# Four part reads of the scores' blocks, and one block transposition in place of two, in an RWKV-7 trunk layer

## The chip, the cores and the metric

The kernel runs on one core of one Trainium2 chip. The metric is device time in microseconds (us) of one execution, as the median of several. The engines are named as in the profile: PE (TensorE, matmuls), PEld (its weight loads), DVE (VectorE), ACT (ScalarE), POOL (GpSimd) and SP (SyncE, which issues most of the DMAs). An engine works through its own queue in order; a row of a profile is one instruction or a run of like ones.

## The reference, cut to what matters

One layer of a residual trunk over 512 tokens and 2048 features, all in float32. Half of the features go through 16 RWKV-7 heads of 64, the other half through a pooling branch; both are gated, projected, added to the residual, gated again by a per-layer embedding and normalised.

```python
h = rms_norm(x, norm_g[i]);  z = h @ w_in[i]              # 512 x 2048 by 2048 x 6272
zs = zs + (token_shift(zs) - zs) * mu[i]                   # r, k, v, two lora inputs
decay = exp(-exp(-softplus(-(w0 + tanh(wd) @ w_up)) - 0.5));  a = sigmoid(a0 + ad @ a_up)
kk = k * k_k;  kk = kk / max(norm(kk per head), KK_EPS);  k = k * (1 + (a - 1) * k_a)
# per head, per token t:
sa  = S @ -kk_t
S   = S * w_t + sa kk_t a_t + v_t k_t;   y_t = S @ r_t
y = head_group_norm(y) + bonus;  y_rwkv = y * silu(g_rwkv)
d = causal_multiscale_pool(u);   y_pool = (d @ w_pool) * pool_scale * silu(g_pool)
x = x + concat(y_rwkv, y_pool) @ w_out
x = x + sigmoid(x @ w_pg + b_pg) * (p @ w_ple);   return rms_norm(x, final_g)
```

## The kernel before, in words

Every large product is done as three products of float32r halves (`whi`, `wlo` of a weight; `hhi`, `hlo` of the activations), so each weight tile that SP loads (`raw`, 256 KB, four buffers) is split by ACT (`whi`, line 132) and then by DVE (`wlo`, line 133) before PE can use it. The buffers of `raw` come free when `wlo` is made, those of `whi` when PE has used them: the split of one chunk therefore waits on ACT until PE is through with the chunk four before it.

The 16 heads are worked as eight pairs, j = 0 to 7, of 128 partitions. The sequence is cut into eight chunks of 64 tokens, and the token recurrence is turned into a chunk recurrence. For a pair there are these stages, and they overlap across pairs:

- `prepare_key(j)` and `norm_key(j)`: the squared key `kk` is split into `kqh` (ACT, line 140) and `kql` (DVE, line 141), and two matmuls `pss` with the block matrix `blk` sum it per head: the first reads `kqh`, the second `kql`. For j of 2 and more this is done inside `recur(j - 2)`, `pss` at its chunk 5, and ACT copies the sum out (line 576).
- `scores(j)`: 32 matmuls `pm` and four masked copies `mt`; then the 32x32 diagonal blocks of the strictly triangular matrices are written to DRAM (`nd`, four DMAs, line 677) and read back as `n32`, two tiles of 16 rows each (`n` in the rows), in which each of four groups of 32 partitions holds the same 32 blocks (line 682). After them SP has `load_ab` (`ur`, `ar`), `bg` and `vg` for later stages.
- `invert(j)`: DVE inverts the 32 blocks by 31 steps of a multiply `tm` (line 709) and an add `xw` (line 713). The first tile of `n32` is needed by the first step, the second by step 16. For j of 1 and more the steps are handed out a few at a time within `recur(j - 1)`, and DVE's queue has other work behind each. The result goes to DRAM (`xd`) and back into `x1` (four DMAs, line 724).
- `gather(j)`: the corner blocks of `x1` are transposed on DVE (`y1`, line 777) and PE forms the off-diagonal blocks of the inverse: 32 small matmuls `pq`, one reading each block and head, then `pmv` and `px`.
- `recur(j)`: for each of eight chunks a chain PE `py`, DVE `zs` (line 844), PE `pu`, ACT `uv` (line 858), PE `ps`, DVE `sbd` (lines 872 and 874), and again. Between the links PE gets `pump(n)` matmuls of the input projections `zk`, `zr`, `zv`, `zg`, `zb` as filling.

After the last pair come the output projection (`acc_o`), the gate projection (`acc_g`) and the closing norm, where PE alone sets the pace.

Who sets the order: PE's instructions are pinned to the order of the code until the last pair is done. Those of DVE, ACT and SP are put into their queues by the framework's planner when the program is built, by its own estimate of when each can begin; `issue_after` holds one instruction behind another, `high_priority` lifts the links of the chain. So an edit of a DMA or of one instruction can move others of the same queue. SP uses its DMA semaphores in turn, and its rows show waits for an earlier DMA's landing before a later issue.

Of the kernel before, what the change touches and what calls it, by code (L numbers as in the profile page):

```python
# [34 lines left out]
def trunk_kernel(ctx: ExitStack, tc: tile.TileContext, x, p, norm_g, w_in, mu, w0, w_up, a0, a_up,  # L35
                 k_k, k_a, r_k, ln_w, ln_b, w_pool, pool_scale, w_out, w_ple, w_pg, b_pg, final_g, out):
    nc = tc.nc
    PSUM = bass.MemoryType.PSUM
    x, p, w_in, w_out, w_ple, w_pg = x[0], p[0, 0], w_in[0], w_out[0], w_ple[0], w_pg[0]
    out = out[0]  # L40
# [118 lines left out]
    def mm(*a, **k):  # L159
        i = nc.tensor.matmul(*a, **k)  # L160
        return tc.keep_in_program_order(i) if pin[0] else i

    def tr(*a):
        i = nc.tensor.transpose(*a)
        return tc.keep_in_program_order(i) if pin[0] else i
# [30 lines left out]
    n_ = 0  # L196
# [13 lines left out]
    for kind, nm, j in jobs:  # L210
# [7 lines left out]
        else:  # L218
            g, i = j // 4, j % 2
# [79 lines left out]
    for d in range(KT):  # L299
        xt_half(0, d)  # L300
        if d in WPOS:
            c = len(wl_)
# [18 lines left out]
    for g, win in enumerate(WINDOWS):  # L321
        t_ = cst.tile([P, win], F32, name=f"rc{g}")
# [61 lines left out]
    for nm, rows in (("u", slice(0, 64)), ("a", slice(64, 128))):  # L384
# [3 lines left out]
        t_ = rw.tile([P, T], F32R, name=f"{nm}hh")  # L388
# [257 lines left out]
    def scores(j):  # L646
        ar, bk, v_ = (st_[j][n_] for n_ in ("ar", "bk", "v_"))
        kph, kpl = st_[j].pop("kp")

        mt = rw.tile([P, 2, 8, 2, C], F32, name=f"mt{j}", tag="mt", bufs=2)  # L650
        pm = [[psM.tile([P, T], F32, name=f"pm{j}_{par}0", tag="m"),
               psY.tile([P, T], F32, name=f"pm{j}_{par}1", tag="y")] for par in range(2)]
        for par in range(2):
            for q in range(4):
                for h in range(2):
                    rows = slice(64 * h, 64 * h + 64)
                    mm(pm[par][h][:, q * P:(q + 1) * P], bk[rows, q, 2 * par:2 * par + 2, :],
                       ar[rows, q, 2 * par:2 * par + 2, :], start=True, stop=True)
        for par in range(2):
            for h in range(2):  # L660
                nc.vector.tensor_tensor(mt[:, par, h::2, :, :],
                                        pm[par][h].rearrange("p (u a t) -> p u a t", u=4, a=2),
                                        msk[:, par:par + 2, :].unsqueeze(1).to_broadcast([P, 4, 2, C]), ALU.mult)


        ps = psM.tile([P, T], F32, name=f"pbo{j}", tag="m")
        mm(ps, blk, kph, start=True, stop=False)
        mm(ps, blk, kpl, start=False, stop=True)
        bv = rw.tile([P, T], F32, name=f"bv{j}", tag="bv", bufs=2)
        nc.vector.tensor_tensor(bv, ps, v_, ALU.mult)  # L670

        nd = dram.tile([2, 2, 8, 32, 32], F32, name=f"nd{j}", tag="nd")
        for par in range(2):
            pb = 64 * (1 - par)
            for b in range(2):
                rows = slice(pb + 32 * b, pb + 32 * b + 32)
                nc.sync.dma_start(out=nd[par, b].rearrange("u r c -> r u c"),
                                  in_=mt[rows, par, :, 1 - par, 32 * b:32 * b + 32])
        nb = []
        for i in range(2):  # L680
            t_ = rw.tile([P, 16, 32], F32, name=f"n32{j}_{i}", tag=("kk", "kp")[i])
            n_ = nc.sync.dma_start(out=t_, in_=nd[:, :, :, 16 * i:16 * i + 16, :].rearrange(
                "a b u r c -> (a b u) r c").unsqueeze(0).to_broadcast([4, 32, 16, 32]))
            nb.append(t_)
        if j + 1 < NJ:
            with tc.issue_after(n_.ins):
                load_ab(j + 1)
        bg = rw.tile([P, NCH, 4, 32], F32, name=f"bg{j}", tag="bk")
        with tc.issue_after(n_.ins):
            for q in range(4):  # L690
                nc.sync.dma_start(out=bg[32 * q:32 * q + 32],
                                  in_=st_[j]["bkd"].rearrange("(b k) (c q i) -> q k c b i", b=4, q=4, i=32)[q])
        if j:
            vg, vd = vgs[j]
            with tc.issue_after(n_.ins):
                for q in range(4):
                    nc.sync.dma_start(out=vg[32 * q:32 * q + 32],
                                      in_=vd.rearrange("(b k) (c q i) -> q k c b i", b=4, q=4, i=32)[q])
        st_[j].update(mt=mt, nb=nb, bv=bv, bg=bg)
# [30 lines left out]
    def gather(j):  # L730
        d = st_[j]
        v_, mt = d.pop("v_"), d["mt"]
        if j + 1 < NJ:
            if j == 0:
                prepare_key(1)
            decay_and_rate(j + 1)

        uv = rw.tile([P, NCH, P], F32, name=f"uv{j}", tag="uv")
        if j:
            vg, _ = vgs.pop(j)  # L740
            for h in range(2):
                hr = slice(64 * h, 64 * h + 64)
                nc.vector.transpose(uv[hr, h::2, :].rearrange("p c (b k) -> p c b k", k=32), vg[hr])
        else:
            ps = psY.tile([P, T], F32, name=f"pv{j}", tag="y")
            for tt in range(NT):
                tr(ps[:, tt * P:(tt + 1) * P], v_[:, tt * P:(tt + 1) * P], ident)
            pv = ps.rearrange("p (t c) -> p t c", c=P)
            nc.scalar.copy(uv[0:64, 0::2, :], pv[0:64])
            nc.scalar.copy(uv[64:128, 1::2, :], pv[64:128])  # L750


        if j == 0:
            turn_key(0, 0)
            turn_key(0, 1)
        pump(H4)

        d.update(uv=uv)
        if j == 0:
            norm_key(1)  # L760
        if 0 < j < NJ - 1:
            with tc.issue_after(read[-1].ins):
                spread_norm(j + 1)
        pump(H5)
        pump(HX)

        x1 = d["x1"]

        def units(fn):
            for u in range(8):  # L770
                for par in range(2):
                    fn(u, par, 64 * (1 - par))

        y1 = rw.tile([P, 8, 32], F32, name=f"y1{j}", tag="tm")

        with tc.issue_after(late[0].ins):
            yt = [nc.vector.transpose(y1[pb:pb + 32], x1[pb:pb + 32, :, 0:32]) for pb in (0, 64)]
        with tc.issue_after(yt[0].ins), tc.issue_after(yt[1].ins):
            if normed:
                normed.pop()()  # L780
            if j + 1 < NJ:
                scale_key(j + 1)
        ps3 = psM.tile([P, 8, 32], F32, name=f"pq2{j}", tag="m")
        units(lambda u, par, pb: mm(ps3[pb + 32:pb + 64, u, :],
                                                  mt[pb:pb + 32, par, u, 1 - par, 32:64],
                                                  y1[pb:pb + 32, u, :], start=True, stop=True,
                                                  tile_position=(pb, pb + 32)))
        q2t = rw.tile([P, 8, 32], F32, name=f"q2{j}", tag="xw")
        with tc.high_priority(offset=HP):
            for pb in (0, 64):  # L790
                nc.scalar.copy(q2t[pb + 32:pb + 64], ps3[pb + 32:pb + 64])
        psv = psM.tile([P, 8, C], F32, name=f"pmv{j}", tag="m")
        units(lambda u, par, pb: mm(psv[pb:pb + 64, u, :], mt[64 - pb:128 - pb, par, u, 1 - par, :],
                                    uv[64 - pb:128 - pb, 2 * (u // 2) + par, 64 * (u % 2):64 * (u % 2) + 64],
                                    start=True, stop=True))
        ps4 = psM.tile([P, 8, 32], F32, name=f"px2{j}", tag="m")
        units(lambda u, par, pb: mm(ps4[pb:pb + 32, u, :], q2t[pb + 32:pb + 64, u, :],
                                                  x1[pb + 32:pb + 64, u, 32:64], start=True, stop=True,
                                                  tile_position=(pb + 32, pb)))
        for pb in (0, 64):  # L800
            nc.scalar.copy(x1[pb:pb + 32, :, 32:64], ps4[pb:pb + 32])
        mv = rw.tile([P, 4, P], F32, name=f"mv{j}", tag="mv")
        nc.scalar.copy(zsp[0][64:128, :].rearrange("p (h t) -> p h t", h=2), psv[64:128, 0:2, :])
        nc.scalar.copy(mv.rearrange("p q (h t) -> p (q h) t", h=2), psv)
        d["mv"] = mv
        pump(H1)
        if pending:
            gates.append(pending.pop()())
        pump(H1)
# [150 lines left out]
    prepare(0)  # L960
    pump(H3)
    scores(0)
    pump(H2)
    for _ in invert(0):
# [3 lines left out]
    for j in range(NJ):  # L968
# [6 lines left out]
        if j + 1 == NJ:  # L975
            pn.append(rw.tile([P, 2, T // 32, 32], F32, name="pn", tag="ar", bufs=2))
            for q in range(4):
                for c in range(2):
                    nc.sync.dma_start(out=pn[0][32 * q:32 * q + 32, c],
                                      in_=p[:, c * P + 32 * q:c * P + 32 * q + 32].rearrange("(b k) i -> k b i", k=32))  # L980
# [93 lines left out]
    for ec in range(D // EC):  # L1074
# [3 lines left out]
        for tt in range(NT):  # L1078
            rows = slice(tt * P, (tt + 1) * P)
            t_ = pp.tile([P, EC], F32, name=f"x2_{ec}_{tt}", tag=("u", "sw")[tt // 2])  # L1080
# [3 lines left out]
                                in_=t_.rearrange("p (c e) -> p c e", e=P))  # L1084
# [204 lines left out]
```

## Time and profile before

| what | before |
|---|---|
| median of 3 runs | 1072.54 us (1072.24 to 1074.22) |
| the profiled execution, its own time | 1077.76 us |
| its span, first to last instruction | 1076.0 us |
| mean granted TensorE clock | 0.997 |
| PE busy | 1047.7 us, 97% |
| DVE busy | 711.7 us, 66% |
| ACT busy | 435.0 us, 40% |
| PE busy in 0 to 27 us | 15.09 us |
| PE busy in 702 to 1076 us | 365.26 of 374 us |

The profiled execution is 5.22 us over the median of the runs, and 1.76 us of its time lies outside the span. A timeline row gives the start, the length, the engine, the line, the operation, out<-in, the shapes and the count; the bracket at its end is the idle time of that engine just before and what ended it. A row of the table of waits gives the sum, the number of times and the longest wait.

### The profile page before, as it was taken

Reading aid. Unit: us, or ns where it says so; the run is one execution under the profiler, and the core shown is the slowest. Engines: PE = TensorE matmul, PEld = TensorE weight load, DVE = VectorE, ACT = ScalarE, POOL = GpSimd, SP = SyncE. Lnnn points to the kernel's source line nnn. Section 1 sums busy time; section 2 is a strip of 40 time slices with the busy share of each in tenths; the row PEclk is TensorE's granted clock in tenths of the full one; section 3 lists DMA queues with packets and bytes.
Section 4 is the critical chain, followed back from the end, with each engine's and each line's share of the span. In section 5 each row is a group of like instructions: output and inputs, shape, how many; then the busy total and the mean of one; then the engine's idle time right before and its main releaser. Section 6 shows DMA issues by size and latency. Waiting matters only on the chain.

```text
span 1076.0 us, 17131 instructions
## 1 busy us (share of the span) xinstructions
PE 1047.7 (97%) x5912; PEld 864.6 (80%) x5912; DVE 711.7 (66%) x1879; ACT 435.0 (40%) x893; POOL 72.6 (7%) x180
## 2 busy tenths in 40 slices
PE   5999999999999999999999999999999999999996
PEld 4888878888877887888888788888888888888885
DVE  6676968878688689687786977464353344435356
ACT  7633424434334345253443344544232232324337
POOL 2100011010110110101101201000000000000000
PEclk9999999999999999999999999999999999999998
DMA  7434453453443544534544453775747659454534
GB/s 237 110 115 101 135 132 95 130 139 99 143 116 100 160 105 128 128 95 133 132 118 133 112 130 108 225 259 163 183 152 190 163 145 272 129 177 159 173 98 157
DMA packets 272733, 155.41 MB, mean 144 GB/s; under 512 B 114449, under 2 KB 235386, under 8 KB 272646
## 3 DMA queue, kind: packets, MB, share of 16 engines
q1 hardware_dynamic: 244630, 125.74, 42.2%
q10 hardware_dynamic: 28016, 28.58, 8.8%
q8 instruction: 46, 0.75, 0.3%
q14 instruction: 41, 0.34, 0.1%
HBM read 128.79 MB, written 24.95 MB: 143 GB/s over the span
## 4 chain that ended last, share of the span: by engine, by line
PE 81%; DVE 9%; DMA 5%; ACT 2%; issue 2%; SPq 1%; ACTq 0%; DVEq 0%
PE acc_o L160 16%; PE acc_g L160 16%; PE zb L160 10%; PE zv L160 7%; PE zr L160 7%; PE zg L160 6%; PE zk L160 6%; PE py L160 2%; PE pple L160 2%; DMA n<-nd 1%; PE pu L160 1%; PE pm L160 1%; DMA x<-xd 1%; PE pp L160 1%; PE ps L160 1%
## 5 line engine op out<-in xcount | busy, mean ns | idle before, releaser
L133 DVE TENSOR_TENSOR wlo_g<-raw_g,whi_g 128x512 fp32r<-128x512 f32 x84 | 57.1, 687 | 76.0 <-ACT whi_g L132 73.8
L160 PE MATMUL zb<-hhi,whi_b 128*128 128x512 f32 x256 | 105.5, 412 | 0.0
L160 PE MATMUL zb<-hhi,wlo_b 128*128 128x512 f32 x256 | 100.4, 392 | 0.0
L160 PE MATMUL zb<-hlo,whi_b 128*128 128x512 f32 x256 | 99.8, 390 | 0.0
L160 PE MATMUL acc_o<-wlo_o,yhi 128*128 128x512 f32 x256 | 99.6, 389 | 0.0
L160 PE MATMUL acc_o<-whi_o,ylo 128*128 128x512 f32 x256 | 99.6, 389 | 0.0
L133 DVE TENSOR_TENSOR wlo_o<-raw_o,whi_o 128x512 fp32r<-128x512 f32 x64 | 43.9, 690 | 81.0 <-ACT whi_o L132 72.8
L160 PE MATMUL acc_o<-whi_o,yhi 128*128 128x512 f32 x256 | 94.7, 389 | 0.0
L132 ACT CAST whi_g<-raw_g 128x512 fp32r<-128x512 f32 x84 | 51.9, 620 | 103.0 <-PE acc_g L160 57.4
L160 PE MATMUL acc_g<-whi_g,x2hi 128*128 128x512 f32 x208 | 81.1, 390 | 0.0
L160 PE MATMUL acc_g<-wlo_g,x2hi 128*128 128x512 f32 x208 | 81.0, 389 | 0.0
L160 PE MATMUL acc_g<-whi_g,x2lo 128*128 128x512 f32 x208 | 80.7, 390 | 0.0
L881 POOL TENSOR_SCALAR s0p<-sbd,pw 64x64 f32<-64x64 f32 x96 | 56.4, 587 | 336.6 <-DVE sbd L874 245.1
L132 ACT CAST whi_o<-raw_o 128x512 fp32r<-128x512 f32 x64 | 39.5, 621 | 96.1 <-PE acc_o L160 55.0
L132 ACT CAST whi_b<-raw_b 128x512 fp32r<-128x512 f32 x64 | 39.6, 620 | 75.9 <-PE zb L160 22.4
L713 DVE TENSOR_TENSOR xw<-xw,tm 128x60 f32<-128x60 f32 (+24 forms) x248 | 52.2, 210 | 7.1
L160 PEld LDWEIGHTS zb<-hhi,wlo_b 128*128 128x128 f32 x256 | 48.0, 188 | 10.8
L160 PEld LDWEIGHTS acc_o<-whi_o,ylo 128*128 128x128 f32 x256 | 48.1, 188 | 10.1
L160 PEld LDWEIGHTS acc_o<-whi_o,yhi 128*128 128x128 f32 x256 | 48.0, 188 | 10.0
L160 PEld LDWEIGHTS acc_o<-wlo_o,yhi 128*128 128x128 f32 x256 | 48.0, 188 | 9.9
L133 DVE TENSOR_TENSOR wlo_b<-raw_b,whi_b 128x512 fp32r<-128x512 f32 x64 | 43.7, 684 | 17.8 <-ACT whi_b L132 17.2
L160 PEld LDWEIGHTS zb<-hhi,whi_b 128*128 128x128 f32 x256 | 48.2, 188 | 8.6
(289 smaller groups left out, 2502.2 us busy)
## 6 DMA issues: line engine op xcount, KB each, us to landing
raw_b<-in_w_in_dram SPq DMA_DIRECT2D x64, 256.0 KB
raw_o<-in_w_out_dram SPq DMA_DIRECT2D x64, 256.0 KB
raw_g<-in_w_pg_dram SPq DMA_DIRECT2D x64, 256.0 KB
raw_k<-in_w_in_dram SPq DMA_DIRECT2D x32, 256.0 KB
raw_r<-in_w_in_dram SPq DMA_DIRECT2D x32, 256.0 KB
raw_v<-in_w_in_dram SPq DMA_DIRECT2D x32, 256.0 KB
raw_g<-in_w_in_dram SPq DMA_DIRECT2D x32, 256.0 KB
bkd<-bk SPq DMA_DIRECT2D x8, 512.0 KB
```

Of the source, the lines that this page charges most:

```text
L132: made.append(nc.scalar.copy(hi, raw))
L133: made.append(nc.vector.tensor_tensor(lo, raw, hi.bitcast(F32), ALU.subtract))
L160: i = nc.tensor.matmul(*a, **k)
L713: nc.vector.tensor_tensor(xw[:, 0:n_, s + 1:32], xw[:, 0:n_, s + 1:32], tm[:, 0:n_, 0:w_], ALU.add)
L881: nc.gpsimd.tensor_scalar(s0p[hc, :], nxt[hc, hc], pcn[hc], None, ALU.mult)
```

## The change

Two edits. In `scores`, each of the two reads of `nd` that fill 128 partitions by a broadcast over four groups is replaced by four reads of 32 partitions each with the same source. In `gather`, the two transpositions of 32 partitions each (of partitions 0 to 31 and 64 to 95) are replaced by one over all 128; the half of its output that is new is read by nothing.

```diff
@@ scores
             t_ = rw.tile([P, 16, 32], F32, name=f"n32{j}_{i}", tag=("kk", "kp")[i])
-            n_ = nc.sync.dma_start(out=t_, in_=nd[:, :, :, 16 * i:16 * i + 16, :].rearrange(
-                "a b u r c -> (a b u) r c").unsqueeze(0).to_broadcast([4, 32, 16, 32]))
+            for q in range(4):
+                n_ = nc.sync.dma_start(out=t_[32 * q:32 * q + 32], in_=nd[:, :, :, 16 * i:16 * i + 16, :].rearrange(
+                    "a b u r c -> (a b u) r c"))
@@ gather
-            yt = [nc.vector.transpose(y1[pb:pb + 32], x1[pb:pb + 32, :, 0:32]) for pb in (0, 64)]
-        with tc.issue_after(yt[0].ins), tc.issue_after(yt[1].ins):
+            yt = nc.vector.transpose(y1, x1[:, :, 0:32])
+        with tc.issue_after(yt.ins):
```

The line numbers behind line 682 are one higher in the changed kernel. PE's and POOL's queues keep their order. In the other three the planner has moved instructions; three places follow.

SP's queue at `scores(3)`; `n` are the reads, `raw_r` and `raw_v` weight chunks, `ur` a lora weight. Before:

```order
L677 DMA nd_3715<-mt_3685 32x8x32 x4
L129 DMA raw_r_2_2113<-in_w_in_dram 128x4x128
L682 DMA n_0_3720<-nd_3715 128x1x512
L682 DMA n_1_3722<-nd_3715 128x1x512
L357 DMA ur_3724<-in_w_up_dram 64x128 x2
L129 DMA raw_r_3_2119<-in_w_in_dram 128x4x128
```

and now:

```order
L677 DMA nd_3730<-mt_3700 32x8x32 x4
L129 DMA raw_r_2_2124<-in_w_in_dram 128x4x128
L683 DMA n_0_3735<-nd_3730 32x512 x3
L129 DMA raw_r_3_2130<-in_w_in_dram 128x4x128
L683 DMA n_0_3735<-nd_3730 32x512
L683 DMA n_1_3740<-nd_3730 32x512 x2
L129 DMA raw_v_0_2156<-in_w_in_dram 128x4x128
```

The last quarter of the first tile now stands behind a weight chunk. So it does in every pair but one: in `scores(1)` all four stand ahead of the chunk.

ACT's queue in `recur(0)`, around `norm_key(2)`; `kqh` is the high half of the squared key, `kk<-pss` the copy of the sum. Before:

```order
L132 CAST whi_v_0_1316<-raw_v_0_1314 128x512
L140 CAST kqh_2094<-kk_2092 128x512
L858 COPY uv_1458<-pu_5_2131 64x64 x2
L132 CAST whi_v_1_1334<-raw_v_1_1332 128x512
L576 COPY kk_2092<-pss_2160 128x512
```

and now:

```order
L132 CAST whi_v_0_1322<-raw_v_0_1320 128x512
L859 COPY uv_1464<-pu_5_2142 64x64 x2
L132 CAST whi_v_1_1340<-raw_v_1_1338 128x512
L140 CAST kqh_2105<-kk_2103 128x512
L576 COPY kk_2103<-pss_2171 128x512
```

`kqh` has moved behind the `uv` copies and the next split of a weight, to just ahead of the copy that reads its matmuls' sum. The same has happened in `recur(1)` to `recur(5)`; in `recur(2)` and `recur(3)` it is also behind the ACT pass of the shifted `sr`. On DVE `kql` has moved along, from behind the split `wlo_v_0` to behind `wlo_v_1` (in `recur(2)` behind DVE's `sr` as well), just ahead of the `sbd` of that chunk.

DVE's queue at `gather(0)`. Before:

```order
L574 TENSOR_SCALAR kk_1429<-pss_1489 128x512
L777 STREAM_TRANSPOSE y_1548<-x_1150 32x256 x2
L595 RECIPROCAL kk_1429<-kk_1429 128x512
L133 TENSOR_TENSOR wlo_b_2_1065<-raw_b_2_1062,whi_b_2_1064 128x512
L133 TENSOR_TENSOR wlo_b_3_1159<-raw_b_3_1156,whi_b_3_1158 128x512
L373 SCALAR_TENSOR_TENSOR sv_1523<-zv_1383,prm,sv_1523 128x511
```

and now:

```order
L574 TENSOR_SCALAR kk_1435<-pss_1495 128x512
L614 TENSOR_SCALAR tha_1462<-tha_1462 128x512
L615 TENSOR_TENSOR ar_1641<-sr_1386,pw_1454 128x4x2x64
L617 TENSOR_TENSOR bk_1642<-kp_1643,ipw_1455 128x4x2x64
L133 TENSOR_TENSOR wlo_b_2_1071<-raw_b_2_1068,whi_b_2_1070 128x512
L618 SCALAR_TENSOR_TENSOR ar_1641<-sk_1286,dprm,pw_1454 128x4x128
L133 TENSOR_TENSOR wlo_b_3_1165<-raw_b_3_1162,whi_b_3_1164 128x512
L373 SCALAR_TENSOR_TENSOR sv_1529<-zv_1389,prm,sv_1529 128x511
L778 STREAM_TRANSPOSE y_1554<-x_1156 128x256
L595 RECIPROCAL kk_1435<-kk_1435 128x512
```

The transposition has gone behind seven instructions, among them `sv`, which needs the last matmul of `zv`. In the later pairs the one transposition stands close to where the second one stood, by at most a few rows ahead or behind.

## The prediction

> **What bounds the kernel now.** I read the head of the page first, then the table of waits, then the chain of waits in the stretches that the table pointed to, then the timelines of single engines there.
>
> ```profile
> span 1076.0 us, 17131 instructions
> PE 1047.7 (97%) x5912; PEld 864.6 (80%) x5912; DVE 711.7 (66%) x1879; ACT 435.0 (40%) x893; POOL 72.6 (7%) x180
> ...
> 0.00:27.00 27.00, 15.09 (x85) 12.38 (x86) 18.40 (x50) 20.69 (x48) 6.44 (x54) 1.00 0.75 236
> 702.00:1076.00 374.00, 365.26 (x1634) 302.37 (x1632) 175.23 (x286) 132.65 (x237) 0.00 (x0) 0.99 0.58 172
> ```
>
> The last two rows are from the view by windows (the stretch, its length, busy PE, PEld, DVE, ACT and POOL, the granted clock). PE is busy for all but 28.3 us of the span, and 27.00 - 15.09 = 11.9 of those fall ahead of 27 us and 374.00 - 365.26 = 8.7 behind 702 us, which the change does not reach. So it can win only from the few short stalls of PE between, and it loses one for one wherever it makes PE stop. The table of waits names those stalls (sum, times, longest):
>
> ```profile
> PE py L160 <- DVE sbd L874: 3.1, 4, 1.6
> PE pq L160 <- DVE y L777: 2.0, 4, 0.7
> PE pu L160 <- DVE zs L844: 1.4, 3, 0.8
> PE pq L160 <- DVE nt L153: 0.4, 1, 0.4
> DVE tm L709 <- DMA n<-nd: 22.9, 8, 5.2
> ```
>
> The first four sum to 6.9 us: all that the two edits could win if everything near them came free. The last says that DVE stands still for 22.9 us at the reads that the change splits. The 6.9 can only be what of this and of the transpositions reaches PE.
>
> **The reads.** Rows of the chain of waits (start, length, what): the broadcast read against an unbroadcast DMA of as many bytes (256 KB) into 128 partitions, and against a read in four parts with the same short runs of 128 bytes.
>
> ```profile
> 287.57 8.56 DMA n<-nd
> 334.93 2.85 DMA raw_g<-in_w_in_dram
> 259.52 4.10 DMA x<-xd
> ```
>
> What is slow is neither the bytes nor the row of DRAM written just before, but this form of read. The Trainium skill (DMA: Bandwidth & Descriptors, Rules for kernel authors) says that a leading zero-stride broadcast of c copies confines a DMA to at most c engines, so here to 4 of 16; the trace agrees as far as 8.56 against 2.85 goes. Each of the four new reads fills 32 partitions once, as a plain read does, so I price them by the lower two rows: 2.85 to 4.10 from the issue to the landing.
>
> The issues, at `scores(3)`:
>
> ```profile
> 287.57 1.17 SPq L682 DMA_DIRECT2D n<-nd  x2
> 290.21 0.76 SPq L129 DMA_DIRECT2D raw_r<-in_w_in_dram  x1
> 289.33 0.67 DVE L133 TENSOR_TENSOR wlo_k<-raw_k,whi_k 128x512 fp32r<-128x512 f32 x1
> ```
>
> An issue of `n` takes 1.17/2 = 0.59. Three parts go out by 287.57 + 3 x 0.59 = 289.3. The weight chunk that now stands ahead of the fourth waits for its buffer, which this `wlo_k` frees at 289.33 + 0.67 = 290.0, and its row shows the issue at 290.21; so the fourth part goes out at 290.4 to 290.8 and lands at 293.3 (with 2.85) to 294.9 (with 4.10), in place of 287.57 + 8.56 = 296.1. The last part is therefore 1.2 to 2.8 earlier although the read has been split around another DMA. PE's stalls behind it:
>
> ```profile
> 298.92 0.49 PE L160 MATMUL py<-sbd,ar 128*128 128x128 f32 x2 [1.60 <-DVE sbd L874]
> 152.03 0.38 PE L160 MATMUL py<-sbd,ar 128*128 128x128 f32 x1 [0.70 <-DVE sbd L874]
> 154.32 0.38 PE L160 MATMUL pu<-zs,x 128*128 128x128 f32 x1 [0.40 <-DVE zs L844]
> 591.70 0.38 PE L160 MATMUL py<-sbd,ar 128*128 128x128 f32 x1 [0.55 <-DVE sbd L874]
> 140.26 0.49 PE L160 MATMUL pu<-zs,x 128*128 128x128 f32 x2 [0.84 <-DVE zs L844]
> ```
>
> The first comes 2.8 behind the landing, through one step of the inverse, two `wlo` and the `sbd` that PE waits for; the next three stand behind the landings of `scores(1)` (twice) and `scores(7)` in the same way. I take all four as gone: 1.60 + 0.70 + 0.40 + 0.55 = 3.25. The last, 0.84, is not behind a read but behind DVE's queue at `gather(0)` and after, which is shorter by up to 5.2 + 0.43 once DVE is not held at the first reads (the longest wait for `n`) and one transposition (0.43, below) is gone: gone too, 0.84. In the pairs not named DVE's waits shrink as well, but PE does not stop for them; nothing is won there.
>
> The price of the split is six more issues a pair, 6 x 0.59 = 3.5 us of SP, which push the weight chunks back. PE's waits hold no row for a weight after the start, and SP comes free earlier on the other side (it waits for the landing of slow reads eight issues back). I cost it at nothing; if that cover is gone, a chunk is late by up to 3.5 us, and it would show as `zr` or `zv` waiting on `wlo`.
>
> **The transposition.** One of 0.43 is saved eight times, 3.5 us of DVE, and PE waits for the last of each two at four gathers only.
>
> ```profile
> L777 DVE STREAM_TRANSPOSE y<-x x16: 423/434/436, 120.0 to 634.9; 32x256 f32<-32x256 f32 x16
> 341.75 0.44 PE L160 MATMUL pq<-y,mt 32*32 32x32 f32 x16 [0.73 <-DVE y L777]
> 415.87 0.69 PE L160 MATMUL pq<-y,mt 32*32 32x32 f32 x30 [0.65 <-DVE y L777]
> 119.58 0.69 ACT L372 ACTIVATE sv<-zv,dprm 128x512 f32<-128x512 f32 x1
> 121.09 0.50 PE L160 MATMUL pq<-y,mt 32*32 32x32 f32 x20 [0.32 <-DVE y L777]
> ```
>
> Its length on 128 partitions is not in the trace: at least that of one on 32 with the same 256 elements a partition (0.43), at most four of them (1.74). I take 0.43, since DVE's 128-partition rows are as long as their elements per partition. `gather(3)` wins 0.73 (there the first `pq` need just the other transposition, and DVE is free), `gather(4)` 0.43 of 0.65, `gather(2)` the 0.4 of the `nt` row, which is queued behind the second one. `gather(0)` loses: the transposition is now behind DVE's `sv`, which follows ACT's: 119.58 + 0.69 + 0.75 (as `sr` has on DVE, below) + 0.43 = 121.45, and `pq` resumes with a short latency at 121.6 rather than at 121.09: -0.5. Sum 1.06. With 1.74 a transposition, all four would be lost and each gather would be later by 0.9.
>
> So the gains are 3.25 + 0.84 + 1.06 = 5.2 us.
>
> **The wait that the change adds.** The order of ACT and DVE has moved `kqh` and `kql` in six pairs. Before, at `norm_key(2)` (ACT, DVE, PE in turn):
>
> ```profile
> 167.30 0.61 ACT L140 CAST kqh<-kk 128x512 fp32r<-128x512 f32 x1
> 169.10 0.62 ACT L132 CAST whi_v<-raw_v 128x512 fp32r<-128x512 f32 x1 [0.73 <-PE zr L160]
> 170.49 0.59 ACT L576 COPY kk<-pss 128x512 f32<-128x512 f32 x1 [0.76 <-PE pss L160]
> 168.04 0.68 DVE L141 TENSOR_TENSOR kql<-kk,kqh 128x512 fp32r<-128x512 f32 x1
> 169.83 0.39 PE L160 MATMUL pss<-kqh,blk 128*128 128x512 f32 x1
> 170.06 0.39 PE L160 MATMUL pss<-kql,blk 128*128 128x512 f32 x1
> ```
>
> The split `whi_v` at 169.10 waits for PE to be through with a `zr`, and PE comes to `pss` 0.73 later. `kqh` was long done; now it is behind this split, which no faster DMA can bring forward. ACT: 169.10 + 0.62 + 0.61 = 170.33, so the first `pss` starts 0.5 late. DVE: `wlo_v` from 169.72, 0.68, then `kql`, 0.68: 171.08, and the second `pss` starts 1.0 later than at 170.06. What is behind PE there is the pumped work, so the whole product stream shifts by 1.0. The copy `kk<-pss` of `norm_key(3)`, `(5)` and `(7)` has the same idle of 0.76 ahead of it, so the split is as close there:
>
> ```profile
> 241.68 0.59 ACT L576 COPY kk<-pss 128x512 f32<-128x512 f32 x1 [0.76 <-PE pss L160]
> 390.21 0.59 ACT L576 COPY kk<-pss 128x512 f32<-128x512 f32 x1 [0.76 <-PE pss L160]
> 534.73 0.59 ACT L576 COPY kk<-pss 128x512 f32<-128x512 f32 x1 [0.76 <-PE pss L160]
> ```
>
> In `norm_key(4)` and `(6)` the split starts with `pss` itself, and in (4) `sr` is ahead of `kqh` and `kql` too:
>
> ```profile
> 315.31 0.62 ACT L132 CAST whi_v<-raw_v 128x512 fp32r<-128x512 f32 x1 [1.26 <-PE zr L160]
> 315.96 0.69 ACT L372 ACTIVATE sr<-zr,dprm 128x512 f32<-128x512 f32 x1
> 317.46 0.75 DVE L373 SCALAR_TENSOR_TENSOR sr<-zr,prm,sr 128x511 f32<-128x511 f32 x1
> 315.58 0.39 PE L160 MATMUL pss<-kql,blk 128*128 128x512 f32 x1
> 461.49 0.62 ACT L132 CAST whi_b<-raw_b 128x512 fp32r<-128x512 f32 x1 [0.54 <-PE zv L160]
> 461.75 0.39 PE L160 MATMUL pss<-kql,blk 128*128 128x512 f32 x1
> ```
>
> (4): ACT's `sr` ends at 316.65, DVE's at 316.65 + 0.75 = 317.40, `kql` at 318.08, against 315.58: 2.5. (6): 461.49 + 0.62 + 0.68 + 0.68 = 463.47 against 461.75: 1.7. Loss: 4 x 1.0 + 2.5 + 1.7 = 8.2.
>
> **The sum** is 8.2 - 5.2 = +3.0: the profiled execution goes from its own 1077.76 to 1080.8. It lies 5.22 over the median shown; the terms are short stalls, the same in each execution, so I add them to the median: 1072.54 + 3.0 = 1075.5. Ends of the loss: 4.8 if only `kqh` is waited for (4 x 0.5, 1.7 and 1.1) and 9.6 if one more split of 0.68 stands ahead of `kql` in two of the six. Ends of the gain: 6.9 (all four rows) and 2.5 (`scores(1)` 1.1, 1.2 of `scores(3)`, `gather(3)` less `gather(0)`, no 0.84). Net: -2.1 to +7.1.
>
> **Rivals.**
>
> *They cancel.* DVE is less behind than before, so `kql` may slip in ahead of `wlo_v` by the time at which its inputs come, and PE would wait for `kqh` alone: 4.8 - 5.2 = -0.4, 1072.1. Against it: each engine works its queue in order, and `kql` is queued behind that split. For it: 0.99 hangs on two DVE passes following at once upon ACT's.
>
> *Faster.* The `pss` wait does not reach the end: PE has it on its queue, but what PE does next in the recurrence waits for DVE anyway, and the stalls of the recurrence shrink by as much as `pss` delays PE. It decides if the links `sbd` and `zs` are later than PE by at least 1.0 at these chunks. The `py` row's four waits in all eight pairs speak against that. Then -5.2: 1067.3.
>
> *The parts gain nothing.* Each lands late, since four reads of the same DRAM rows are worked off one behind the other: the 8.56 stays, the 3.25 is not won, and +6.2 follows: 1078.8. For it: the fourth goes out 2.8 later than the broadcast did. Against it: the four parts of `x<-xd` landed within 4.10. The Trainium skill (DMA: Bandwidth & Descriptors, Rules for kernel authors) says of two transfers to disjoint partition halves that they serialize, and that small transfers should be coalesced, which would speak against the split; of these reads no row shows it yet.
>
> **How the numbers follow.** Forecast 0.57, its own range 1074 to 1077.5; cancel 0.24; faster 0.13; parts gain nothing 0.06. The range of 1070.0 to 1079.5 is the net of the ends, -2.1 to +7.1, put on 1072.54 and rounded outward below; it leaves out the faster rival and the tails. A measurement of this kernel can tell about 0.2%, 2.1 us, from no change. Of the forecast's 0.57 some 0.45 lies over +2.1 and 0.12 within; of cancel's 0.24, 0.18 lies within, 0.04 below and 0.02 above; with the other two: faster 0.17, same 0.30, slower 0.53.
>
> **What would show it.** In the chain of waits after, `n<-nd` should be gone or under 5 us, and the row of DVE's waits for it down from 22.9 to under 8. New rows of PE's waits should read `pss` behind DVE `kql`, six times, 8 us or less, 2.5 the longest, and behind ACT `kqh`. The row `py` behind `sbd` should fall to under 1, `pq` behind `y` to about 1, with `gather(0)` the longest. I am wrong if `pss` has no such row (then faster), if `n` still lands 7 us behind its first issue, or if the transposition on 128 partitions takes much over 0.43.

## The result, and the profile after

The changed kernel takes 1080.66 us by the median (1079.97 to 1082.38, 6 runs) against 1072.96 us before: 1.0075 of the time before, with a 95% interval of 1.0062 to 1.0088, or +7.7 us. Slower was forecast, but 1075.5, in a range of 1070.0 to 1079.5.

The page of the profile after (span and busy times), and the rows of its table of waits that answer to those shown of before (sum, times, longest):

```profile
span 1078.3 us, 17225 instructions
PE 1048.5 (97%) x5912; PEld 863.6 (80%) x5912; DVE 708.7 (66%) x1871; ACT 436.4 (40%) x893; POOL 72.4 (7%) x180
...
PE pss L160 <- ACT kqh L140: 4.0, 6, 1.7
PE pss L160 <- DVE kql L141: 2.0, 6, 0.4
PE py L160 <- DVE sbd L875: 0.2, 1, 0.2
PE pq L160 <- DVE y L778: 1.1, 2, 0.7
PE pu L160 <- DVE zs L845: 0.6, 2, 0.4
DVE tm L710 <- DMA n<-nd: 2.4, 5, 0.9
```

Each part of the change shows as forecast: DVE waits 2.4 us for the reads in place of 22.9, `py` behind `sbd` has gone from 3.1 to 0.2, and `pss` has six new waits each for `kqh` and for `kql`. At `norm_key(2)` (ACT, DVE and PE in turn):

```profile
166.43 0.62 ACT L132 CAST whi_v<-raw_v 128x512 fp32r<-128x512 f32 x1 [0.73 <-PE zr L160]
166.96 0.61 ACT L140 CAST kqh<-kk 128x512 fp32r<-128x512 f32 x1
167.09 0.69 DVE L133 TENSOR_TENSOR wlo_v<-raw_v,whi_v 128x512 fp32r<-128x512 f32 x1 [0.20 <-ACT whi_v L132]
167.69 0.69 DVE L141 TENSOR_TENSOR kql<-kk,kqh 128x512 fp32r<-128x512 f32 x1
167.63 0.50 PE L160 MATMUL pss<-kqh,blk 128*128 128x512 f32 x1 [0.30 <-ACT kqh L140]
168.44 0.51 PE L160 MATMUL pss<-kql,blk 128*128 128x512 f32 x1 [0.31 <-DVE kql L141]
```

The split waits for `zr`, `kqh` and `kql` follow it, and PE stands still twice. The bracket of a PE row counts only the idle time behind the modelled end of the matmul before it; what the stream loses is seen better from starts. PE runs its instructions in the same order in both kernels, so the start of each can be set against its fellow in the other trace. The table gives the steps at which the difference changes (us, my sums from the starts), against the profiled execution that the prediction was made from:

| place | forecast | after less before |
|---|---|---|
| `pss` at `norm_key` 2, 3, 4, 5, 6, 7 | 1.0, 1.0, 2.5, 1.0, 1.7, 1.0: +8.2 | 1.05, 1.04, 2.49, 1.16, 1.78, 1.09: +8.6 |
| `py` and `pu` behind the reads, pairs 1, 3, 7 | -3.25 | -1.43, -1.76, -0.71: -3.9 |
| `pu` behind `zs` at 140 | -0.84 | -0.4 |
| `pq` at the gathers | -1.06 | -1.45 |
| sum, with small steps | +3.0 | +2.2 |

So between the two traces the sum holds, at +2.2 against +3.0: the profiled execution after has an own time of 1079.97 against 1077.76. That it is so close is in part luck, since its four terms are off by 0.4 to 0.7 each, in both directions. What does not hold is the step from there to the medians, which are 7.7 apart. Of the 5.5 us between, 4.8 lie in the execution before, whose profile stood that far over the median of 1072.96, and 0.7 in the execution after, which stood that much under its own. The experiments begin with the first.

### The profile page after: what moved, and what is told of

It is laid out like the page before. It is cut to its first block, busy times and chain, and to the rows that moved or that the text cites. A ratio compares the mean times of both kernels' runs of the same rounds, so it can differ in the third digit from the quotient of the medians.

```text
span 1078.3 us, 17225 instructions
## 1 busy us (share of the span) xinstructions
PE 1048.5 (97%) x5912; PEld 863.6 (80%) x5912; DVE 708.7 (66%) x1871; ACT 436.4 (40%) x893; POOL 72.4 (7%) x180
```

## The experiments

**The kernel before, profiled again.** No edit.

> The kernel before, unchanged, profiled beside its own timed runs. Instruction by instruction on PE the changed kernel ended 2.2 us later than the profiled execution of before, but its median is 7.7 us later than the median of before: the profiled execution of before stood 4.8 us over its median. Theory A (that one execution was long in itself, and the profile and the median of one kernel are otherwise the same): own time of the new profile within 2 us of its median, 1071 to 1075, and the 4.8 us are found as shorter stalls or rows in some stretch. Rival B (a profile always adds about 5 us to this kernel, and not to the changed one): 1076 to 1079 in the profile again, with a median at 1073.

Median 1073.04 us (11 runs), own time of the new profile 1072.90. Page, waits, and the rows of PE at the three places where it stalled in the first execution:

```profile
span 1071.2 us, 17131 instructions
...
DVE tm L709 <- DMA n<-nd: 16.3, 8, 3.6
PE pq L160 <- DVE y L777: 1.7, 3, 0.7
PE pu L160 <- DVE zs L844: 0.7, 2, 0.5
PE py L160 <- DVE sbd L874: 0.2, 1, 0.2
...
149.98 0.38 PE L160 MATMUL py<-sbd,ar 128*128 128x128 f32 x2
294.59 0.49 PE L160 MATMUL py<-sbd,ar 128*128 128x128 f32 x2
586.70 0.42 PE L160 MATMUL py<-sbd,ar 128*128 128x128 f32 x2
```

Theory A holds: no bracket stands behind these `py`, and their row in the table of waits has gone from 3.1 to 0.2 in one and the same kernel. Instruction by instruction the first execution is 4.86 us later on PE than this one, in these steps: +0.39 at the first `pq`, +0.34 at `pu` at 140, then +1.44 (`py` 0.87 and `pu` 0.57) at pair 1, +1.76 at pair 3 and +0.71 at pair 7, and the rest in steps of 0.1 to 0.2. The steps at pairs 1, 3 and 7 are the stalls that the prediction counted as gains of the reads, and the 0.34 is part of what it counted as the gain of `zs`: of the 0.84 ahead of that `pu`, 0.50 is left in this execution. What differs is when the first tile of `n` has landed. The table has it in us after its first issue, from the updates of the DMA's semaphore in the trace: the fourth that comes with data for a broadcast read, and for the changed kernel the sixteenth of the last of the four parts to land.

```
pair                      0     1     2     3     4     5     6     7
first execution        7.88  8.44  7.33  8.56  7.20  6.65  6.63  7.53
this execution         6.26  6.11  7.47  6.81  6.89  6.38  6.91  6.75
changed kernel         5.60  3.49  6.10  5.59  5.87  5.70  7.15  5.50
```

In this execution PE waits for none of them. The changed kernel against this execution: `pss` +8.6, the gathers -1.2, the reads 0, in all +7.1.

**The reads alone.** The kernel before with the first edit of the change and not the second.

```diff
+            for q in range(4):
+                n_ = nc.sync.dma_start(out=t_[32 * q:32 * q + 32], in_=...)
```

> Only the reads are split; the two transpositions stay. The moved kqh and kql are all in this kernel too. Theory A (the loss is the wait at pss, 8.6 us by the steps of PE between the two traces; the transposition wins about 1.4): pss waits as in the changed kernel, median 1 to 2 us over it, 1081.5 to 1083, ratio to before 1.008 to 1.010. Rival (the one transposition on 128 partitions is what makes DVE late): 1074 to 1077, ratio near 1.003.

1082.16 us, ratio 1.0088 (1.0074 to 1.0101), as theory A has it. Waits:

```profile
PE pss L160 <- ACT kqh L140: 4.0, 6, 1.7
PE pss L160 <- DVE kql L141: 2.0, 6, 0.4
DVE tm L710 <- DMA n<-nd: 2.5, 6, 0.8
```

The two `pss` rows are those of the changed kernel to the digit, so it is the split of the reads that moves `kqh` and `kql`, and its whole cost is there. PE's steps against the second execution of before are again 8.6 at `pss`, +0.3 at `gather(0)` and -0.7 at `gather(2)`, and none at the reads.

**The transposition alone.** The kernel before with the second edit only.

```diff
-            yt = [nc.vector.transpose(y1[pb:pb + 32], x1[pb:pb + 32, :, 0:32]) for pb in (0, 64)]
+            yt = nc.vector.transpose(y1, x1[:, :, 0:32])
```

> Only the transpositions are joined; the reads are the broadcast ones. kqh and kql stand where they stood before. Theory A: no wait at pss, n lands 7 to 9 us after its issue, the stalls of py behind sbd as before, pq behind y shorter by 1 to 1.5 us in sum: median 1071 to 1073, ratio 0.998 to 1.000. Rival (the transposition carries the loss): slower by 3 us or more, ratio over 1.003.

1070.68 us, ratio 0.9983 (0.9974 to 0.9991): faster than both kernels. Waits, and the group of the transpositions (least, median and greatest ns):

```profile
DVE tm L709 <- DMA n<-nd: 14.9, 6, 4.3
PE pq L160 <- DVE y L777: 0.7, 1, 0.7
...
L777 DVE STREAM_TRANSPOSE y<-x x8: 438/442/446, 118.3 to 627.0; 128x256 f32<-128x256 f32 x8
```

One block transposition on 128 partitions takes 442 ns where one on 32 took 434 (there were two), and `gather(0)` loses nothing, as `y` keeps its place ahead of `sv`. PE's steps: -0.74 at `gather(2)`, -0.89 at `(3)`, -0.48 at `(4)`, +0.13 at `(6)`, +0.31 at `(7)`: -1.7. Theory A had the time nearly right and the reads wrong: the first tiles landed after 6.2 to 7.0 us, not 7 to 9, and `py` behind `sbd` waits 0.2 us, not the 3.1 of the first execution. DVE still waits 14.9 us for the slow reads here, in six pairs, and PE for none of that.

**Both parts, and `kqh` and `kql` back in their places.** The changed kernel with other buffers for the halves of the squared key.

```diff
-        kqh = rw.tile([P, T], F32R, name=f"kqh{j}", tag="t", bufs=4)
-        kql = rw.tile([P, T], F32R, name=f"kql{j}", tag="t", bufs=4)
+        kqh = rw.tile([P, T], F32R, name=f"kqh{j}", **(dict(tag="tha") if j > 1 else dict(tag="t", bufs=4)))
+        kql = rw.tile([P, T], F32R, name=f"kql{j}", **(dict(tag="ipw") if j > 1 else dict(tag="t", bufs=4)))
```

> Both parts of the change, and kqh and kql of pairs 2 to 7 take the buffers of tha and ipw, idle there, in place of two of the four that they share with vg and others; nothing is computed otherwise. With that the planner puts kqh and kql back right behind the split ahead of which they stood before. Theory A (the loss of the change is the moved kqh and kql): no wait at pss, the gains stay, the changed kernel less 8.6: 1071 to 1073 by the median, ratio 0.998 to 1.001. Rival C (part of the 7.7 lies in what the trace of before does not show, such as SP's added issues or the shorter rows of DRAM traffic): PE's steps at pss gone, but the median stays at 1076 or over.

1071.78 us, ratio 0.9990 (0.9981 to 0.9999): the 7.7 us are gone. Waits, and the transposed corners' first use in two gathers:

```profile
ACT kk L576 <- PE pss L160: 3.1, 4, 0.8
PE py L160 <- DVE sbd L875: 0.2, 1, 0.2
PE pq L160 <- DVE y L778: 2.5, 4, 1.1
...
120.83 0.69 PE L160 MATMUL pq<-y,mt 32*32 32x32 f32 x32 [0.43 <-DVE y L778]
482.44 0.69 PE L160 MATMUL pq<-y,mt 32*32 32x32 f32 x32 [1.07 <-DVE y L778]
```

PE has no row of a wait at `pss` any more; the steps against the changed kernel are -1.05, -1.04, -2.49, -1.15, -1.78 and -1.09, each of them undone. This kernel is still 1.1 us by the medians over the one with the transposition alone. Against that one PE loses 0.50 at `gather(0)`, 0.55 at `(3)`, 0.25 at `(4)` and 0.42 at `(6)`. Only the first of these comes with the split reads: the changed kernel has it too (`y` stands behind `sv`), but not the other three. Those are new in this kernel, where the planner has moved more than `kqh` and `kql` in DVE's queue (at `gather(3)` `y` now stands behind one more weight split). The time of this kernel spreads less, 1071.13 to 1072.43 in 11 runs, where the kernel before, in 11 runs beside it, had 1071.88 to 1075.42. Whether the earlier landing of the reads does that is not shown: the changed kernel, with the same reads, had 1079.97 to 1082.38 in 6 runs.

**The reads made later.** The kernel before with one broadcast read more, into an idle buffer, ahead of the two of each pair.

```diff
+        idle = rw.tile([P, 16, 32], F32, name=f"idle{j}", tag="tha")
+        nc.sync.dma_start(out=idle, in_=nd[:, :, :, 0:16, :].rearrange(
+            "a b u r c -> (a b u) r c").unsqueeze(0).to_broadcast([4, 32, 16, 32]))
```

> The kernel before, with one more broadcast read of the same 16 rows put into an idle buffer ahead of the two reads of each pair, so that the first tile lands later; kqh, kql and the transpositions stand as before. Two executions of the kernel before differed by 4.86 us on PE, all of it in stalls behind the first tile: it landed after 8.44, 8.56 and 7.53 us at pairs 1, 3 and 7 in the long one, after 6.11, 6.81 and 6.75 in the other, where PE did not stop. Theory D (there is slack for a landing of about 6.8 us, and what is over it goes to PE one for one): with a landing 3 to 6 us later PE stops at pairs 1, 3 and 7 by 3 to 6 us each, and at some of the others: slower by 9 to 30 us, ratio 1.008 to 1.028, in py behind sbd and pu behind zs. Rival (the late landing only came with something else that held PE): under 3 us, ratio under 1.003.

1088.37 us, ratio 1.0148 (1.0134 to 1.0162): theory D, though the first tile came only 1.9 to 3.4 us later than in the second execution of before, and the stops at pairs 1, 3 and 7 are 1.9 to 2.2. Waits, three rows of the chain of waits (start, length, what), `py` at pair 3, and two rows of the view by windows, the second right behind that `py` (the granted clock is third from the end):

```profile
DVE tm L712 <- DMA n<-nd: 35.3, 8, 6.1
PE py L160 <- DVE sbd L877: 10.1, 8, 2.0
...
289.23 8.39 DMA n<-nd
366.46 8.69 DMA n<-nd
440.47 8.18 DMA n<-nd
...
300.39 0.49 PE L160 MATMUL py<-sbd,ar 128*128 128x128 f32 x2 [2.04 <-DVE sbd L877]
...
299.00:301.00 2.00, 0.61 (x4) 0.56 (x5) 1.84 (x7) 0.00 (x0) 1.26 (x2) 1.00 0.44 125
301.00:303.00 2.00, 2.00 (x7) 1.51 (x6) 1.83 (x9) 0.62 (x1) 0.00 (x0) 0.52 0.91 242
```

Now the chain runs through the read in six of the eight pairs. The read proper is issued some 0.63 us behind the added one, which stands where the read stood; counted from there, the landing less the step of PE at `py` gives the slack that PE has at each pair. Pair 3: 8.39 + 0.63 = 9.02, less 2.20, is 6.8; from the first execution of before it is 8.56 - 1.76 = 6.8. Pair 7: 9.02 - 2.19 = 6.8 and 7.53 - 0.71 = 6.8. Pair 1: 9.48 - 1.88 = 7.6 and 8.44 - 0.87 = 7.6. The slack is 6.8 at pair 5 as well and 8.3 to 8.4 at 2, 4 and 6. Two executions in which the reads landed at quite different times thus give the same three slacks, and beyond them a late landing goes to the start of that `py` one for one. I had put pair 1 at 6.8 too, which was too little by 0.8. At pairs 3 and 7 PE then lost some 1.5 us more in the work behind `py`: the granted clock was 0.50 for 3.4 us there, from 301.1 and from 601.4, and rows of the product stream took 0.63 us in place of 0.39. The stalls ahead were 2.04 and 2.03 us long; behind the 1.87 of pair 5 the clock stayed at 1.00. No run tried what sets this.

**`kqh` and `kql` late, alone.** The kernel before, reads and transpositions as they were, with the two held behind the six splits by hand.

```diff
+    BEHIND = {2: "v2_1", 3: "v3_2", 4: "v4_3", 5: "b4_0", 6: "b5_1", 7: "b6_2"}
...
+            with tc.issue_after(wall[BEHIND[j]][1].ins), tc.issue_after(wall[BEHIND[j]][2].ins):
+                split(kqh, kql, kk)
```

> The kernel before, reads and transpositions unchanged, with kqh and kql of pairs 2 to 7 held behind the weight splits behind which they stand in the changed kernel (not behind sr at norm_key(4)). Theory A: six waits at pss with PE steps of 1.04 to 1.2 at pairs 2, 3, 5 and 7, 1.8 at 6 and 1.8 at 4 (2.5 with sr): 7.8 us, median 1079.5 to 1081.5, ratio 1.0060 to 1.0080. Rival (the moved key costs that much only together with the split reads, which put SP and DVE into another rhythm): under 4 us, ratio under 1.004.

1081.32 us, ratio 1.0084 (1.0070 to 1.0098): within theory A's 1079.5 to 1081.5, and just over its ratio of 1.0080. Waits, and a row of the chain of waits:

```profile
PE pss L162 <- ACT kqh L142: 3.3, 6, 1.0
PE pss L162 <- DVE kql L143: 1.9, 6, 0.4
...
438.38 8.00 DMA n<-nd
```

The steps at `pss` are 1.04, 1.04, 1.74, 1.16, 1.78 and 1.09, 7.85 us of the 8.8 by the medians: the moved key by itself carries the loss. The profiled execution of this kernel is again a long one, 1085.14 against its median of 1081.32, and again it is the reads: at pair 5 the tile landed after 8.00 and PE's step at `py` is 1.22, with the slack of 6.8 found there above.

**The reads as two broadcasts over two groups each.**

```diff
+            for q in range(2):
+                n_ = nc.sync.dma_start(out=t_[64 * q:64 * q + 64], in_=... .to_broadcast([2, 32, 16, 32]))
```

> The kernel before, with each read split into two of 64 partitions, each a broadcast over two groups. A measure of the read by itself. If the number of copies in a read sets its pace, each of the two, with half of the bytes, lands no sooner than the one of 256 KB did (6 to 7.5 us). If the bytes set it, each lands after 3.5 to 4.5 us. PE is not expected to show more than the kernel before unless kqh moves here too: within 0 to +9 us.

One execution at 1082.43 us. Waits, and a row of the chain of waits:

```profile
DVE tm L710 <- DMA n<-nd: 29.6, 8, 5.7
PE py L160 <- DVE sbd L875: 6.0, 5, 1.6
...
143.74 8.19 DMA n<-nd
```

The first of the two reads of a tile landed 5.5 to 6.3 us after its own issue, with half of the bytes of the one that took 6.1 to 7.5; the second 7.5 to 8.2 after its own. That is neither quite of the two: nearer to a pace set by the copies (6 to 7.5) than to one set by the bytes (3.5 to 4.5), and the tile is complete later than before, 8.1 to 8.8 us after its first issue. PE has no wait at `pss` here; its steps at `py` are 1.42, 1.78, 1.64 and 1.56 at pairs 1, 3, 5 and 7. Counted as above that gives slacks of 7.4, 6.4, 6.7 and 6.8, within 0.4 of those found there.

## Why the prediction was wrong, point by point

**The direction and the loss were right.** The step "the wait that the change adds" gave 8.2 for six waits at `pss`; the trace has 8.6, the kernel with that move alone 7.85 (without `sr` at `norm_key(4)`), and taking the move back wins it all. Of the single terms, those of `norm_key(2)`, `(3)`, `(4)` and `(6)` came within 0.1, and those of 5 and 7 were 0.16 and 0.09 low. For `kqh` alone, the low end, the prediction put 1.7 and 1.1 at (4) and (6), where the first `pss` moved by 1.86 and 1.20. The accuracy of the six followed from reading which instruction the moved one is now queued behind, and what that one waits for: a split that PE itself releases 0.73 us before it comes to `pss`.

**The step that failed** is the last of the sum: "the terms are short stalls, the same in each execution, so I add them to the median". They were not. The gains of the reads, 3.25, and of `zs`, 0.84, were read from an execution that stood 5.22 us over the median, and the stalls behind the reads are most of what it stood over it by. In the second execution of before PE has no stall at any of the four rows behind the reads, and the changed kernel gains nothing against it there. Of the 0.84 ahead of `pu` 0.50 is left in that execution and 0.44 in the changed kernel, so this one was not won either. Without them the forecast is 8.2 - 1.06 = +7.1, 1079.7, where 1080.66 was measured; the trace against the second execution of before has the same +7.1. The prediction named the 5.22 and did not ask where they were.

**That the reads would land earlier was right**; that this is worth something to PE was right only against an execution in which they landed late. The last part of the first tile was to land 1.2 to 2.8 us earlier at `scores(3)`, at 5.7 to 7.3 after the first issue; it landed at 5.59, 2.67 after its own issue, where 2.85 to 4.10 was the price. SP's queue there in the changed kernel, and the first step of the inverse:

```profile
286.61 1.29 SPq L683 DMA_DIRECT2D n<-nd  x3
289.09 0.39 SPq L129 DMA_DIRECT2D raw_r<-in_w_in_dram  x1
289.53 1.43 SPq L683 DMA_DIRECT2D n<-nd  x3
292.32 0.19 DVE L710 TENSOR_TENSOR tm<-i,n 128x31 f32<-128x31 f32 x1
```

An issue takes 1.29/3 = 0.43, not the 0.59 used, and the fourth part is held by the weight chunk as read from the order, yet DVE no longer waits at all. But a tile that lands at 5.59 in place of the 6.81 of the second execution is worth nothing to PE, which has 6.8 to 8.4 of slack. DVE's 22.9 us of waits for the reads were 16.3 in that execution, and PE waited for none of them.

**The transposition.** Forecast -1.06; measured -1.7 alone, and -1.2 with the reads split, where `gather(0)` loses the 0.5 forecast. 0.43 for 128 partitions held (0.434 after), so the bound of 1.74 was far off.

**The rivals.** "Parts gain nothing", given 0.06, came to 1078.8 for another reason: it took the 8.56 to stay, and the three parts at `scores(3)` with no chunk ahead of them had landed by 2.6 to 3.2 us after the first issue. Its sum, which is without the 3.25, comes nearest to what happened all the same. "Cancel" fell with `kql`, which PE waits for in all six places (2.0 us in the table, 0.3 to 0.4 each), and "faster" with `kqh` (4.0). The Trainium skill (DMA: Bandwidth & Descriptors, Rules for kernel authors) says that transfers to disjoint partition halves serialize and are not worth making; in this case's trace the parts did not hold one another up (the three landed 2.64, 2.55 and 2.33 after their own issues, which were 0.4 to 0.5 apart), and the one read that they replace, a broadcast, was the slow one (6.8 and 8.6 there).

**Left open.** With buffers of their own `kqh` and `kql` went back to their places, so the planner's late place for them came from the buffers that they shared; which of the other users of those four buffers it took to be late was not tried. Nor was it tried to put `y` ahead of `sv` with the split reads, which by the steps above I estimate at 0.5.

## What to carry to other kernels

Before a gain is read off a stall, set the profiled execution's time against the median: if it is longer, the stalls to be won may be just that excess, and a second profile of the same kernel, or the spread of like rows in one (here eight equal reads that landed after 6.6 to 8.6 us), tells. A long wait of an engine behind a DMA is worth what the end of the path lacks in slack and no more; slack can be measured by making the transfer later, with an eye on the granted clock behind the stall. And an edit of a DMA is an edit of every queue that a planner orders: look in the new order for instructions that now stand behind one which the bounding engine releases late.

## What the runs showed of the hardware

Eight equal broadcast reads of 256 KB landed after 6.1 to 7.5 us in one execution and after 6.6 to 8.6 in another of the same kernel, and the stalls behind them are 3.9 of the 4.86 us between the two on PE; I had not expected one kernel's time to hang on it. Where a read was late enough to stop PE, the delay was mostly in the last of its four updates: 6.54 and then 8.44 us at pair 1, 6.12 and 8.56 at pair 3, 6.41 and 7.53 at pair 7.

About 1 us after its issue a broadcast read raised its semaphore once, and after that four times with four groups (in the two executions of before not earlier than 5.06 us) and twice with two groups, where half of the bytes took nearly as long. One of the plain parts raised it 16 times, from 1.9 to 2.3 us on for the four of the first tile at `scores(3)`. That agrees with the Trainium skill (DMA: Bandwidth & Descriptors, Why a DMA increments its semaphore by 16 and not by 1), by which only the engines that a DMA uses raise it as their data lands, one step each: four, two and sixteen of them here.
